# Short convolution in groups of four like tiles: norm groups on 32 partitions, summed and spread by VectorE's block transposes

## The chip, the cores and the metric

The kernel runs on one core of a Trainium2 chip. The metric is the device time of one execution in microseconds (us). Below, PE is TensorE (the matrix engine; PEld its weight loads), DVE is VectorE, ACT is ScalarE, POOL is GpSimd, and SP is SyncE, which here only issues DMAs.

## The reference, cut to what matters

The program is one decoder layer on 256 tokens of width 2048: a mixer, a cross attention to 256 memory tokens, a SwiGLU block, and a final norm. All of it is float32. The change is in the short convolution of the mixer and its grouped norm, which has 16 groups of 128 channels:

```python
def grouped_rmsnorm(x, g, n_groups):
    shp = x.shape
    xf = x.astype(jnp.float32).reshape(shp[:-1] + (n_groups, shp[-1] // n_groups))
    xf = xf * lax.rsqrt(jnp.mean(xf * xf, axis=-1, keepdims=True) + NORM_EPS)
    return (xf.reshape(shp) * g.astype(jnp.float32)).astype(x.dtype)

def hybrid_mixer(h, w_in, ssd_conv_w, ssd_conv_b, dt_bias, a_log, d_skip, ssd_norm,
                 sc_conv_w, sc_norm, w_out):
    proj = h @ w_in
    z, xbc, dt_raw, sc_u, sc_b, sc_c = jnp.split(proj, IN_SPLITS, axis=-1)
    ...
    y_ssd = grouped_rmsnorm(y * jax.nn.silu(z), ssd_norm, SSD_GROUPS)
    v = sc_b * causal_dwconv(sc_c * sc_u, sc_conv_w)
    y_sc = grouped_rmsnorm(v, sc_norm, SC_GROUPS)
    return jnp.concatenate([y_ssd, y_sc], axis=-1) @ w_out
```

`sc_u`, `sc_b` and `sc_c` are 2048 columns each; `causal_dwconv` is a depthwise convolution over three tokens. The other branch (SSD, a state space model) has four norm groups of 512 channels.

## The kernel before

**The weight stream.** All weights come from memory once, in chunks of 128x1024 values (512 KB), in a fixed list (`stream_plan`). SP loads a chunk into a raw tile `r`, up to six ahead (`load_to`). `split_to` makes two tiles of it: ACT rounds it to the tile `h` (line 172, type fp32r), and DVE subtracts to get the rest `l` (line 173). Raw tiles have six buffers, `h` and `l` four each, so the cast of a chunk can start when PE is done with the chunk four before it.

**The projections** (`tok_mm`, lines 260 to 262). Tokens stand on the partitions, 512 output columns on the free axis, in two accumulators of 128 tokens. Three products, h by h, h by l and l by h, make up one float32 product, so that a chunk costs 12 matmuls of 128x512. A `unit` is two chunks. The input projection has 22 groups of 512 columns, each of 8 chunks or 4 units; then comes the output projection of the mixer (stage `wo`, 4 column groups of 16 chunks, in the order of `out_order`), and then attention and SwiGLU, which the change leaves alone.

**Turning a group** (`group_post`). When a group's accumulators are full, DVE transposes them in blocks of 32x32 (`turn_blocks`, line 276), SP writes them to scratch memory (`put`), and SP reads them back (`get`) with channels on the partitions and 256 tokens on the free axis: four tiles of 128 channels. The columns of the weights are permuted on the host (`_turned`) so that each tile gets its own 128 channels.

**Processes.** All work on these tiles is written as Python generators. Once in each unit, between its two chunks, `step` moves every live generator on to its next `yield`. PE and SP execute in exactly this order. DVE, ACT and POOL follow an order that a scheduler makes, which is also fixed when the program is built.

**The short convolution.** `mixer_groups` cuts one list into the 22 groups: tiles of the SSD branch (B, C, z, xs) and of the short convolution (scc, scu, scb) are mixed in a group. For each of the 16 channel tiles, `scu_post` multiplies u by c (line 776) and convolves (lines 778 and 781), and `scb_post` multiplies by b (line 788). One tile is one norm group, so the sum of squares runs over the 128 partitions. `norm_group` with `feature_squares` does it: PE transposes the tile (`flip`, line 207, two transposes of 128x128), ACT squares and sums along the free axis (line 234), DVE scales (line 241), POOL raises to the power -0.5 (line 242), PE spreads the result over the partitions (`bcast`, line 249, two more transposes), DVE multiplies (line 749), and ACT and DVE make the hi and lo halves `ys` (lines 192 and 193) that stage `wo` uses.

The four SSD norm groups use the same `norm_group`, with `feature_sums` in place of `feature_squares`.

Of the kernel before, what the change touches and what calls it, by code (L numbers as in the profile page):

```python
# [13 lines left out]
F32 = mybir.dt.float32  # L14
F32R = mybir.dt.float32r
# [5 lines left out]
T = 256  # L21
# [6 lines left out]
EPS = 1e-5  # L28
# [11 lines left out]
NV = _o  # L40

ZT, XT, BT, CT = 0, 16, 32, 36
UT, SBT, SCT = 0, 16, 32


def mixer_groups():

    o = [("B", "a", BT, 0), ("C", "a", CT, 0), ("z", "a", ZT, 0), ("z", "a", ZT + 1, 1)]
    sc = iter(range(16))

    def short_conv():
        j = next(sc)
        return [("scc", "b", SCT + j, j), ("scu", "b", UT + j, j), ("scb", "b", SBT + j, j)]

    for g in range(4):
        if g:
            o += [("B", "a", BT + g, g), ("C", "a", CT + g, g)]
        for t in range(4 * g, 4 * g + 4):
            if t > 1:
                o.append(("z", "a", ZT + t, t))  # L60
            o.append(("xs", "a", XT + t, t))
            if t % 4:
                o += short_conv()
    for _ in range(4):
        o += short_conv()
    return [o[i:i + 4] for i in range(0, len(o), 4)]
# [28 lines left out]
def trunk(tc, wst, vecs, xp, xtp, mp, wdt_in, nfin, outp):  # L95
# [9 lines left out]
    with ExitStack() as ctx:  # L105
# [25 lines left out]
        def tmp(shape=(128, T)):  # L131
            return tp.tile(list(shape), F32, tag="t", name=nm("t"))
# [69 lines left out]
        def flip(src):  # L202

            ps = msc()
            for i, a in enumerate(src):
                for tb in range(2):
                    nc.tensor.transpose(ps[:, i * T + tb * 128:i * T + tb * 128 + 128],  # L207
                                        a[:, tb * 128:tb * 128 + 128], ident)
            return ps

        def small(name):
            return cp.tile([128, 2], F32, tag=name, name=nm(name), bufs=4)
# [12 lines left out]
                                            axis=mybir.AxisListType.XY, op=ALU.add)  # L225
            return e

        def feature_squares(src):

            ps = flip([src])  # L230
            e = small("rv")
            j = tmp()
            for tb in range(2):
                act(j[:, tb * 128:tb * 128 + 128], ps[:, tb * 128:tb * 128 + 128], AF.Square,
                    accum_out=e[:, tb:tb + 1])
            return e

        def inv_rms(e, n):
            r = small("rr")
            with tc.high_priority():  # L240
                ts(e, e, 1.0 / n, EPS, ALU.mult, ALU.add)  # L241
                gtt(r, e, half, op=ALU.pow)  # L242
            return r

        def bcast(r):
# [18 lines left out]
        def side_blocks(tiles, k0):  # L264

            def blocks(i, tb):
                a = tiles[k0 + i]
                return a[:, tb * 128:tb * 128 + 128], a[:, T + tb * 128:T + tb * 128 + 128]

            return blocks  # L270

# [82 lines left out]

        U = cp.tile([128, T], F32, name="U")
        ident = cp.tile([128, 128], F32, name="ident")
        half = cp.tile([128, 2], F32, name="half")

        c0 = VOFF["nmem"] + 16
        wdt = slot()  # L360
# [5 lines left out]
            dst[i] = t  # L366

        nc.gpsimd.memset(half, -0.5)
        act(small("rv"), half, AF.Identity)
# [371 lines left out]
        def norm_group(items, sums, sq, n, key):  # L741
            r = inv_rms(sums(sq), n)
            yield
            yield
            rb = bcast(r)
            yield
            for src, gain, dst in items:
                y = tmp()
                stt(y, src, gain, rb[:, 0:T], ALU.mult, ALU.mult)  # L749
                ys[dst] = hilo(y)  # L750
                if dst % 2:
                    yield
            done(key)
# [12 lines left out]

        scc, scv = {}, {}

        def scc_post(j, src):
            scc[j] = src  # L770
            return
            yield

        def scu_post(j, src):
            u = tmp()
            tt(runs(u), src, scc.pop(j), ALU.mult)
            a = slot()[:, 0:T]
            ts(a, u, v("sw", 3 * j + 2), None, ALU.mult)
            for k in (1, 0):
                d = 2 - k  # L780
                stt(a[:, d:], u[:, 0:T - d], v("sw", 3 * j + k), a[:, d:], ALU.mult, ALU.add)  # L781
            scv[j] = a
            return
            yield

        def scb_post(j, src):
            a = scv[j]
            tt(runs(a), runs(a), src, ALU.mult)
# [8 lines left out]
        paces = len(groups) - 3  # L797

        def group_post(n, accs):
            t = turn_blocks(accs)  # L800
            yield
            w = put(t)
            yield
            d = get(w)
            yield
            for f, (kind, _, _, j) in enumerate(groups[n]):
                p = posts[kind](j, d[:, f])
                if next(p, 0) is None:
                    procs.append(p)
                if f < 3 and n < paces:  # L810
                    yield

        def in_units(n, accs, cs):
# [7 lines left out]
            for n in range(2):  # L821
                in_units(n, first[n], cs)
        for n in range(2, len(groups)):
            for kind, _, _, j in groups[n]:
                if kind == "B":
                    procs.append(decay(j))
            in_units(n, [acc(), acc()], range(0, KT // 2, 2))


# [67 lines left out]
        def wo_post(n, accs):  # L897
            add_to_res(n, accs, h1s)
            if n == 0:
                act(small("rv"), half, AF.Exp)  # L900
# [312 lines left out]
    return a.reshape((n, 4, 4, 32) + rest).swapaxes(1, 2).reshape((n * 512,) + rest)  # L1213


def _cols(a):

    import numpy as np
    a = np.asarray(a)
    n = a.shape[0] // 128  # L1220
    return a.reshape(n, 128, -1).transpose(1, 0, 2).reshape(128, -1)


def _weights(i):
    import numpy as np
    w_in = np.asarray(i["w_in"])[0]
    blk = {}

# [5 lines left out]
    rows = {m: (_turned(np.asarray(i[k])[0]) if m == "d" else np.asarray(i[k])[0]).reshape(-1, 2, 128, i[k].shape[-1] // 512, 512).transpose(3, 0, 2, 1, 4)  # L1234
            for m, k in (("wo", "w_out"), ("o", "w_o"), ("g", "w_gate"), ("u", "w_up"), ("d", "w_down"))}
    groups = []
    for g in mixer_groups():
        c = np.concatenate([w_in[:, (0 if m == "a" else 5152) + 128 * t:][:, 0:128] for _, m, t, _ in g], axis=1)
        c = _turned(c.T).T
# [24 lines left out]

def _vectors(i):
    import numpy as np
    g = {k: np.asarray(a) for k, a in i.items() if a.ndim <= 3}
    part = {
        "nmix": _cols(g["norm_mix"][0]), "nmem": _cols(g["mem_norm"]), "nxa": _cols(_turned(g["norm_xa"][0], 3)),
        "nffn": _cols(g["norm_ffn"][0]), "nssd": _cols(g["ssd_norm"][0]),  # L1270
        "nsc": _cols(g["sc_norm"][0]), "cw": _cols(g["ssd_conv_w"][0].T), "cb": _cols(g["ssd_conv_b"][0]),
        "sw": _cols(g["sc_conv_w"][0].T), "dsk": _cols(np.repeat(g["d_skip"][0], 64)),
        "dtb": np.broadcast_to(g["dt_bias"][0], (128, H)), "alog": np.broadcast_to(g["a_log"][0], (128, H)),
    }
    return np.ascontiguousarray(np.concatenate([part[n] for n, _ in _W], axis=1))
# [33 lines left out]
```

## Time and profile before

| what | value |
|---|---|
| time, median of three runs | 1533.63 us (1533.0 to 1533.98) |
| the profiled execution's own time | 1533.51 us |
| its span, first to last instruction | 1531.8 us |
| granted TensorE clock, mean | 0.999 |
| DVE busy | 928.7 us (61%) |
| ACT busy | 757.9 us (49%) |
| POOL busy | 52.5 us (3%) |
| mean DMA rate | 221 GB/s |

The profile page gives the busy time of each engine, then the span in 40 slices with a digit for the busy share, then the chain of work that ended last: from the last instruction back, at each step to what released it. Its further parts group the instructions by source line. An engine that is busy 99% of the span sets the time; what the other engines do costs something only where that one waits for them. The input projection of the mixer lies between about 57 and 571 us of the span, stage `wo` up to about 747 us.

### The profile page before, as it was taken

To read this page: it belongs to the slowest core of one execution; us is meant where nothing else is said; L and a number is where in the kernel's file an instruction comes from. 1 tells how busy PE (TensorE), PEld (TensorE's weight loads), DVE (VectorE), ACT (ScalarE), POOL (GpSimd) and SP (SyncE) were. 2 spreads that over 40 slices of the span, in tenths; PEclk is the share of its full clock that TensorE was granted. 3 is DMA by queue.
4 is the path that set the end of the run, shared out by engine and by line. 5 is a ranking of instruction groups with operands and counts; after the bars stand their busy time and mean duration, and the time that the engine had idled before them with its cause. 6 is when DMAs were issued, how large, how long until landed. Compare 5 with 4: busy or idle time off the path is not lost.

```text
span 1531.8 us, 18911 instructions
## 1 busy us (share of the span) xinstructions
PE 1518.1 (99%) x6903; PEld 1246.6 (81%) x6903; DVE 928.7 (61%) x1195; ACT 757.9 (49%) x1070; POOL 52.5 (3%) x65
## 2 busy tenths in 40 slices
PE   8999999999999999999999999999999999999997
PEld 6788888788888888888888888888888888888886
DVE  5958778677777766465575555555555555455453
ACT  6665754754654444454465444444444444344343
POOL 0002200100100000000000000000000000000000
PEclk9999999999999999999999999999999999999999
DMA  9787876877867768587535667666666667655562
GB/s 346 256 270 240 260 229 207 280 217 229 269 214 226 233 206 240 199 262 233 192 132 181 223 216 225 219 203 208 221 222 220 222 217 223 226 194 192 193 193 97
DMA packets 141917, 338.34 MB, mean 221 GB/s; under 512 B 12768, under 2 KB 58240, under 8 KB 141824
## 3 DMA queue, kind: packets, MB, share of 16 engines
q1 hardware_dynamic: 132624, 329.74, 66.7%
q10 hardware_dynamic: 9200, 7.39, 1.6%
q8 instruction: 54, 0.88, 0.3%
q14 instruction: 39, 0.32, 0.1%
HBM read 316.06 MB, written 21.02 MB: 220 GB/s over the span
## 4 chain that ended last, share of the span: by engine, by line
PE 96%; DMA 2%; issue 1%; ACT 1%; DVE 0%; SPq 0%; POOLq 0%; POOL 0%; ACTq 0%
PE a L260 30%; PE a L262 30%; PE a L261 30%; DMA r<-in_w_dram 2%; PE a L342 1%; PE m L717 1%; PE a L348 0%; PE m L207 0%; PE m L249 0%; PE a L556 0%; PE m L876 0%; ACT h L172 0%; PE m L701 0%; PE m L719 0%; PE m L935 0%
## 5 line engine op out<-in xcount | busy, mean ns | idle before, releaser
L173 DVE TENSOR_TENSOR l<-r,h 128x1024 fp32r<-128x1024 f32 (+2 forms) x555 | 658.8, 1190 | 534.4 <-ACT h L172 510.0
L172 ACT CAST h<-r 128x1024 fp32r<-128x1024 f32 (+2 forms) x555 | 566.0, 1023 | 693.6 <-PE a L262 619.1
L260 PE MATMUL a<-h,s 128*128 128x512 f32 x2047 | 805.2, 393 | 0.0
L262 PE MATMUL a<-h,s 128*128 128x512 f32 x2047 | 797.8, 390 | 0.0
L261 PE MATMUL a<-l,s 128*128 128x512 f32 x2047 | 797.7, 390 | 0.0
L262 PEld LDWEIGHTS a<-h,s 128*128 128x128 f32 x2047 | 384.3, 188 | 80.9
L260 PEld LDWEIGHTS a<-h,s 128*128 128x128 f32 x2047 | 384.4, 188 | 80.6 <-issue 2.4
L261 PEld LDWEIGHTS a<-l,s 128*128 128x128 f32 x2047 | 384.6, 188 | 77.7
L242 POOL TENSOR_TENSOR rr<-rv,half 128x2 f32<-128x2 f32 x24 | 23.8, 991 | 574.4 <-DVE rv L241 574.3
L658 DVE SCALAR_TENSOR_TENSOR t<-t,vec,t 128x255 f32<-128x255 f32 (+2 forms) x72 | 33.7, 480 | 0.9
L276 DVE STREAM_TRANSPOSE b<-a 128x512 f32<-128x512 f32 x44 | 29.7, 700 | 2.0 <-PE a L262 1.9
L1132 POOL TENSOR_TENSOR fr<-fr,half 128x1 f32<-128x1 f32 x2 | 1.1, 550 | 716.8 <-DVE fr L1131 716.8
L556 PE MATMUL a<-s,h 128*128 128x512 f32 x64 | 23.9, 404 | 1.4 <-DVE s L187 1.1
L1058 ACT ACTIVATE g<-a,fscale 128x512 f32<-128x512 f32 x22 | 15.0, 689 | 9.9 <-PE a L262 9.9
L557 PE MATMUL a<-s,l 128*128 128x256 f32 x64 | 18.4, 287 | 0.8 <-DVE l L173 0.8
L749 DVE SCALAR_TENSOR_TENSOR t<-s,vec,m 128x256 f32<-128x256 f32 x32 | 14.6, 476 | 4.6 <-PE m L249 4.6
L556 PEld LDWEIGHTS a<-s,h 128*128 128x128 f32 x64 | 12.0, 188 | 5.8 <-DVE s L187 2.3
L342 PE MATMUL a<-s,h 128*128 128x512 f32 x64 | 16.5, 400 | 0.0
L781 DVE SCALAR_TENSOR_TENSOR s<-t,vec,s 128x255 f32<-128x255 f32 (+1 forms) x32 | 16.1, 506 | 0.4
L723 DVE SCALAR_TENSOR_TENSOR s<-s,vec,m 128x256 f32<-128x256 f32 x16 | 7.7, 480 | 14.0 <-PE m L719 13.9
L640 ACT ACTIVATE s<-s,nacs 128x256 f32<-128x256 f32 x32 | 16.0, 499 | 0.0
L1066 DVE SCALAR_TENSOR_TENSOR g<-a,fscale,g 128x512 f32<-128x512 f32 x22 | 15.4, 743 | 0.0
(175 smaller groups left out, 629.3 us busy)
## 6 DMA issues: line engine op xcount, KB each, us to landing
r<-in_w_dram SPq DMA_DIRECT2D x535, 512.0 KB, 4.2
w<-b SPq DMA_DIRECT2D x36, 512.0 KB, 3.3
f<-w SPq DMA_DIRECT2D x144, 128.0 KB, 4.5
s<-acsT ACTq DMA_DIRECT2D x24, 256.0 KB, 6.1
s<-in_xt_dram SPq DMA_DIRECT2D x16, 256.0 KB, 6.4
s<-in_x_dram SPq DMA_DIRECT2D x8, 256.0 KB, 7.6
s<-in_m_dram SPq DMA_DIRECT2D x7, 256.0 KB, 7.2
s<-in_nfin_dram SPq DMA_DIRECT2D x4, 256.0 KB, 6.9
```

The lines of the kernel that those rows point to most:

```text
L172: nc.scalar.copy(h[:, c], r[:, c])
L173: tt(l[:, c], r[:, c], h[:, c].bitcast(F32), ALU.subtract)
L242: gtt(r, e, half, op=ALU.pow)
L260: mm(ps[tb], ah, h[:, w], start=start and i == ks[0], stop=False)
L261: mm(ps[tb], ah, l[:, w], start=False, stop=False)
L262: mm(ps[tb], al, h[:, w], start=False, stop=stop and i == ks[-1])
L276: nc.vector.transpose(t[:, tb * 512:tb * 512 + 512], src[tb])
L342: mm(ps, h[:, k * 128:k * 128 + 128], acts[k0 + k], start=start and k == 0, stop=False)
L556: mm(kacc[t], h[:, t * 128:t * 128 + 128], a, start=s, stop=False)
L557: mm(kacc[t][:, 0:T], l[:, t * 128:t * 128 + 128], a[:, 0:T], start=False, stop=e)
L658: stt(a[:, d:], u[:, 0:T - d], v("cw", 4 * ct + k), a[:, d:], ALU.mult, ALU.add)
L781: stt(a[:, d:], u[:, 0:T - d], v("sw", 3 * j + k), a[:, d:], ALU.mult, ALU.add)
```

## The change

1. **Groups of one kind.** `mixer_groups` now makes 10 groups of SSD tiles and 12 groups of the short convolution, each of four tiles of one kind (scc, scu or scb). Two SSD groups come first, then one of each in turn, and the last four are scb, scc, scu, scb. The SSD order within its groups is as before apart from the cut.
2. **Norm groups on 32 partitions.** The columns of the short convolution's groups are no longer permuted on the host. The block transposes then leave norm group b of the four on partitions 32b to 32b+31 of all four tiles. The gains, the convolution's weights and the rows of `w_out` are permuted to match (`_sc_turned`).
3. **Four tiles at a time.** Products, squares, casts and differences of the short convolution take two tiles in one instruction (128x512); the convolution itself and the gains stay at 128x256.
4. **Sums and spreading without PE.** For four tiles together, DVE adds the squares of the four tiles, transposes the sum in blocks of 32x32, and reduces over each 32 columns, which gives 128x8 sums; POOL raises them to -0.5 in one instruction; DVE transposes them back, broadcast, which gives the factor for each token and norm group on its 32 partitions. `feature_squares` is gone, and with it 32 transposes on PE, and the 32 of `bcast` for these groups.
5. **Order of `wo`.** The first two column groups leave chunks 6, 7, 14 and 15 for last, where they left 14 and 15 before.

```diff
-            yield
-            yield
-            yield from norm_group([(a, v("nsc", j), 16 + j)], feature_squares, a, 128, ("sc", j))
+            sq = []
+            for i in range(2):
+                a, ar = pair(scv[n][i])
+                tt(ar, ar, src[:, 2 * i:2 * i + 2], ALU.mult)
+                q = gtp.tile([128, 512], F32, tag="g", name=nm("q"))
+                act(q, a, AF.Square)
+                sq.append(q)
+            yield
+            tt(sq[0], sq[0], sq[1], ALU.add)
+            s = tmp()
+            tt(s, sq[0][:, 0:T], sq[0][:, T:], ALU.add)
+            t = tmp()
+            nc.vector.transpose(t, s)
+            e = cp.tile([128, 8], F32, tag="ge", name=nm("ge"), bufs=2)
+            nc.vector.tensor_reduce(e, runs(t), axis=mybir.AxisListType.X, op=ALU.add)
+            ts(e, e, 1.0 / 128, EPS, ALU.mult, ALU.add)
+            r = cp.tile([128, 8], F32, tag="gr", name=nm("gr"), bufs=2)
+            gtt(r, e, half, op=ALU.pow)
+            yield
+            rb = tmp()
+            nc.vector.transpose(runs(rb), r.unsqueeze(2).to_broadcast([128, 8, 32]))
+            for i in range(2):
+                y = gtp.tile([128, 512], F32, tag="g", name=nm("y"))
+                for f in range(2):
+                    c = slice(f * T, f * T + T)
+                    stt(y[:, c], scv[n][i][:, c], v("nsc", 4 * n + 2 * i + f), rb, ALU.mult, ALU.mult)
+                hi, lo = slot(dt=F32R), slot(dt=F32R)
+                nc.scalar.copy(hi, y)
+                tt(lo, y, hi.bitcast(F32), ALU.subtract)
...
 def out_order():
-    return ([(n, c) for n in range(2) for c in range(14)] + [(n, c) for n in range(2) for c in (14, 15)]
+    late = (6, 7, 14, 15)
+    return ([(n, c) for n in range(2) for c in range(KT) if c not in late] + [(n, c) for n in range(2) for c in late]
             + [(n, c) for n in (2, 3) for c in range(KT)])
```

**On PE**, before, between two chunks of the seventeenth group of the input projection; `a` are the accumulators, `s_639` and `s_678` halves of the normed input, and the row of line 249 is the spreading of one norm group's factor:

```order
L260 MATMUL a_4117<-h_4249,s_639 128x512
L261 MATMUL a_4117<-l_4250,s_639 128x512
L262 MATMUL a_4117<-h_4249,s_639 128x512
L249 MATMUL m_4290<-ident,rr_4196 128x128 x2
L260 MATMUL a_4116<-h_4253,s_678 128x512
L261 MATMUL a_4116<-l_4254,s_678 128x512
L262 MATMUL a_4116<-h_4253,s_678 128x512
```

On PE, after the change, at the same place (lines 242 to 244 are now the three products):

```order
L242 MATMUL a_4027<-h_4137,s_639 128x512
L243 MATMUL a_4027<-l_4138,s_639 128x512
L244 MATMUL a_4027<-h_4137,s_639 128x512
L242 MATMUL a_4026<-h_4141,s_678 128x512
L243 MATMUL a_4026<-l_4142,s_678 128x512
L244 MATMUL a_4026<-h_4141,s_678 128x512
```

The two transposes are gone and the chunks follow on each other. Over the whole program PE has 46 transposes of line 207 and 44 of line 249 before, and 14 and 12 (lines 199 and 231) now; the other matmuls are the same in number.

**On DVE**, before, at about the same place; the row of line 241 scales the sums `rv` that POOL then takes, and that of line 749 uses the factor of the same norm group once PE has spread it; `l` are the halves of weight chunks:

```order
L241 TENSOR_SCALAR rv_4192<-rv_4192 128x2
L173 TENSOR_TENSOR l_4254<-r_4167,h_4253 128x1024
L723 SCALAR_TENSOR_TENSOR s_3917<-s_3917,vec,m_4239 128x256
L173 TENSOR_TENSOR l_4303<-r_4221,h_4302 128x1024
L726 TENSOR_TENSOR s_3917<-s_3917,s_3873 128x256
L734 TENSOR_TENSOR s_3637<-s_3637,t_4287 128x256
L173 TENSOR_TENSOR l_4307<-r_4223,h_4306 128x1024
L658 SCALAR_TENSOR_TENSOR t_4296<-t_4294,vec,t_4296 128x255
L658 SCALAR_TENSOR_TENSOR t_4296<-t_4294,vec,t_4296 128x254
L749 SCALAR_TENSOR_TENSOR t_4348<-s_4033,vec,m_4290 128x256
```

On DVE, after the change, for the third set of four tiles (chunk 160 or so of 176); `q` are the squares, `ge` the sums, `gr` what POOL makes of them, and line 165 is the split of a weight chunk:

```order
L790 TENSOR_TENSOR q_4773<-q_4773,q_4776 128x512
L792 TENSOR_TENSOR t_4820<-q_4773 128x256
L794 STREAM_TRANSPOSE t_4822<-t_4820 128x256
L796 TENSOR_REDUCE ge_4824<-t_4822 128x8
L165 TENSOR_TENSOR l_4786<-r_4708,h_4785 128x1024
L797 TENSOR_SCALAR ge_4824<-ge_4824 128x8
L802 STREAM_TRANSPOSE t_4869<-gr_4827 128x256
L687 TENSOR_TENSOR s_4629<-m_4778,dtn 128x256
L807 SCALAR_TENSOR_TENSOR y_4871<-s_4383,vec,t_4869 128x256
L165 TENSOR_TENSOR l_4834<-r_4756,h_4833 128x1024
```

Where three splits and five other rows stood between the scaling and the use of the factor, line 802, which reads POOL's result, now stands directly behind line 797, which gives POOL its input. It is the same for the fourth set; for the first set one split, and for the second one block transpose and one split stand between the two.

More of the change, by code (lines that the diff above doesn't have):

```diff
@@ L356, in trunk @@
         ident = cp.tile([128, 128], F32, name="ident")
[L357 removed]
+        half = cp.tile([128, 8], F32, name="half")
         c0 = VOFF["nmem"] + 16
@@ L767, in trunk, with pair, scc_post @@
         scc, scv = {}, {}
-        def scc_post(j, src):
-            scc[j] = src
+        def pair(a):
+            return a, a.rearrange("p (f x j) -> p f x j", f=2, x=8)
+        def scc_post(n, src):
+            scc[n] = src
             return
             yield
[L774 to L783, printed above, removed]
-            yield
@@ L805, in group_post @@
             yield
-            for f, (kind, _, _, j) in enumerate(groups[n]):
+            if isinstance(groups[n], tuple):
+                yield from posts[groups[n][0]](groups[n][1], d)
+                return
+            for f, (kind, _, j) in enumerate(groups[n]):
                 p = posts[kind](j, d[:, f])
@@ L823, in trunk @@
         for n in range(2, len(groups)):
-            for kind, _, _, j in groups[n]:
-                if kind == "B":
-                    procs.append(decay(j))
+            for one in [] if isinstance(groups[n], tuple) else groups[n]:
+                if one[0] == "B":
+                    procs.append(decay(one[2]))
             in_units(n, [acc(), acc()], range(0, KT // 2, 2))
@@ L899, in wo_post @@
             if n == 0:
-                act(small("rv"), half, AF.Exp)
+                act(small("rv"), half[:, 0:2], AF.Exp)
             if n == 3:
```

84 lines of the change are left out of this document (45 added, 39 removed).

## The prediction

> **What bounds the kernel now.** I read the page's head, its slices and its chain first, then the waits of PE alone, then the windows.
>
> ```profile
> span 1531.8 us, 18911 instructions
> ...
> PE 1518.1 (99%) x6903; PEld 1246.6 (81%) x6903; DVE 928.7 (61%) x1195; ACT 757.9 (49%) x1070; POOL 52.5 (3%) x65
> ...
> PE   8999999999999999999999999999999999999997
> ...
> PE 96%; DMA 2%; issue 1%; ACT 1%; DVE 0%; SPq 0%; POOLq 0%; POOL 0%; ACTq 0%
> ```
>
> PE is busy in every slice, and the chain that ends last runs on PE for 96% of the span. A high busy share can still hide stalls, so the next view is the list of what PE waited for (total us, times, longest):
>
> ```profile
> PE m L401 <- POOL U L397: 1.8, 1, 1.8
> PE a L556 <- DVE s L187: 1.1, 2, 0.6
> PE a L557 <- DVE l L173: 0.8, 2, 0.6
> PE m L954 <- ACT s L192: 0.6, 1, 0.6
> PE a L556 <- ACT h L172: 0.3, 1, 0.3
> PE m L565 <- ACT h L172: 0.3, 1, 0.3
> PE m L566 <- DVE l L173: 0.2, 1, 0.2
> ```
>
> These are the start of the program (L397 to L567) and attention (L954). No line of the input projection or of stage wo (L260 to L262, L207, L249) is in it. The windows view says the same, as busy time of PE, PEld, DVE, ACT and POOL in a stretch:
>
> ```profile
> 100.00:613.00 513.00, 513.00 (x2375) 416.10 (x2374) 372.96 (x555) 283.07 (x450) 44.47 (x46) 1.00 0.76 237
> 820.00:1260.00 440.00, 440.00 (x1943) 364.43 (x1942) 234.44 (x222) 194.51 (x203) 0.00 (x0) 1.00 0.67 217
> ```
>
> Where the change works, PE is full at granted clock 1.00, and DVE is busy 73% (373 of 513). So a PE instruction less is time less, as long as no other engine comes to hold PE up. The second row is SwiGLU alone, all chunk matmuls: 440/1943 = 0.2264 us from one to the next, and 12 of them, a chunk, last 2.72 us.
>
> **What leaves PE.** The views of the two lines give their count and duration (ns, least/median/most):
>
> ```profile
> L249 PE MATMUL m<-ident,rr x44: 270/272/273, 34.7 to 613.1; 128*128 128x128 f32 x44
> L207 PE MATMUL m<-ident,s x44: 270/272/331, 156.7 to 601.7; 128*128 128x128 f32 x44
> ```
>
> Of each 44, the 16 norm groups of the short convolution own 32; the four SSD groups keep 8, and 4 more serve the input and memory norms. So 64 transposes go, in 32 pairs. What a pair costs is not its duration, since matmuls overlap, but how far it pushes the next chunk matmuls. One pair in the timeline of PE (start, duration):
>
> ```profile
> 421.15 0.39 PE L262 MATMUL a<-h,s 128*128 128x512 f32 x1
> 421.38 0.38 PE L249 MATMUL m<-ident,rr 128*128 128x128 f32 x2
> 421.51 0.48 PE L260 MATMUL a<-h,s 128*128 128x512 f32 x1
> 421.83 0.39 PE L261 MATMUL a<-l,s 128*128 128x512 f32 x1
> ```
>
> Without the pair, L260 and L261 would start 0.226 and 0.453 us after L262, the latter at 421.60. It starts at 421.83: 0.23 us for the pair. The chain of waits agrees, for a pair and for two pairs together:
>
> ```profile
> 310.22 0.22 PE m L249 x2
> ...
> 601.56 0.44 PE m L207 x4
> ```
>
> So 32 pairs cost between 32 x 0.22 = 7.0 and 32 x 0.24 = 7.7 us, the latter if the next matmuls also lose a hundredth or two. I take 0.225 each: **-7.2 us**. Nothing is added on PE.
>
> A rule of the Trainium skill would price this otherwise: "TensorE: Matmul & The Clock Gate", Part 4: PE-mode transpose, gives about 275 ns for a 128x128 transpose within a kernel. This trace's median of 272 ns agrees as a duration; by it as a price the sum would be 64 x 0.275 = 17.6 us, but the 0.11 us that the chain shows for each decides here.
>
> **What comes to DVE, ACT and POOL.** Rows by form (busy us, mean ns):
>
> ```profile
> L173 DVE TENSOR_TENSOR l<-r,h 128x1024 fp32r<-128x1024 f32 x518 | 634.8, 1227 | 519.1 <-ACT h L172 495.5 <-DMA r<-in_w_dram 17.8 <-DMA f<-w 3.1
> L172 ACT CAST h<-r 128x1024 fp32r<-128x1024 f32 x518 | 544.8, 1053 | 672.7 <-PE a L262 609.1 <-issue 27.8 <-DMA r<-in_w_dram 20.6
> L276 DVE STREAM_TRANSPOSE b<-a 128x512 f32<-128x512 f32 x44 | 29.7, 700 | 2.0 <-PE a L262 1.9
> L685 DVE TENSOR_TENSOR s<-s,s 128x512 f32<-128x512 f32 x16 | 10.9, 681 | 0.0
> L193 DVE TENSOR_TENSOR s<-t,s 128x256 fp32r<-128x256 f32 x32 | 12.8, 419 | 0.1
> L749 DVE SCALAR_TENSOR_TENSOR t<-s,vec,m 128x256 f32<-128x256 f32 x32 | 14.6, 476 | 4.6 <-PE m L249 4.6
> L221 DVE TENSOR_REDUCE rv<-m 128x2 f32<-128x256 f32 x4 | 1.7, 422 | 0.6 <-PE m L207 0.5
> L234 ACT ACTIVATE t<-m 128x128 f32<-128x128 f32 x32 | 8.5, 270 | 5.0 <-PE m L207 5.0
> ```
>
> DVE did seven 128x256 instructions and a small one for each tile, about 7 x 0.46 + 0.2 = 3.4 us, 13.7 for four tiles. Now four tiles take seven of 128x512 (0.68 each, 4.8), seventeen of 128x256 (0.42 to 0.48, 7.8), and two half-size transposes, a reduction and a small one (0.35 + 0.35 + 0.42 + 0.2 = 1.3): 13.9. That is no more work over the stage. ACT loses the 32 squarings of L234, done two tiles at a time instead. Neither sum is on the path, because both engines run ahead of PE: the cast of a chunk waits for PE (609 of ACT's 673 us of idle time), since h and l have four buffers each. From that moment PE still has three chunks, 8.2 us, and the cast and the split take 1.05 + 1.23, so a split is ready **5.9 us** before its use. That lead is the cover, and it is gone only if DVE falls back by more.
>
> **The new wait.** DVE's block transpose L802 now stands behind POOL's power of 128x8, close behind the row that feeds POOL, and the splits are queued behind it. The trace has that operation at one and two columns:
>
> ```profile
> L1132 POOL TENSOR_TENSOR fr<-fr,half 128x1 f32<-128x1 f32 x2 | 1.1, 550 | 716.8 <-DVE fr L1131 716.8
> L242 POOL TENSOR_TENSOR rr<-rv,half x24: 688/691/1839, 32.2 to 806.9; 128x2 f32<-128x2 f32 x24
> ```
>
> A second column adds 0.14 us, so eight give 0.55 + 7 x 0.14 = 1.5 us, which I take. The ends are 0.7 (eight columns cost what two do) and 4 x 1.84 = 7.4 (four times a disturbed one). I count DVE's work in the new order with the durations above. The densest place is the first set: among seven splits in a row (7 x 1.23 = 8.6) stand 8 of the 0.48 kind, 5 of 0.68, 7 of 0.42, two whole block transposes and two halves, a reduction and the feeding row (12.9 in all), and the power, beside which one of the splits runs, adds 1.5 - 1.2 = 0.3. That makes 21.8 us, while PE uses seven chunks in 19.0: DVE falls back by 2.8, or by 4.0 if the split has to wait for POOL. At the third set, whose rows stand with the change, nothing runs beside the power: four splits (4.9), 6.8 of other work and 1.5 make 13.2, PE's four chunks 10.9, so 2.3. All of these are under 5.9. The power would have to take 1.5 + 5.9 - 4.0 = 3.4 us at the first set or 1.5 + 5.9 - 2.3 = 5.1 at the third before PE waits; about 4.4 is the mean for the four. So I cost the wait at **nothing**.
>
> That the split might have to wait shows in these two rows of one moment (start, duration), and in the longest split of the stage (ns, least/median/most of all its forms):
>
> ```profile
> 346.05 1.22 DVE L173 TENSOR_TENSOR l<-r,h 128x1024 fp32r<-128x1024 f32 x1 [0.16 <-DMA f<-w]
> 346.06 1.76 POOL L242 TENSOR_TENSOR rr<-rv,half 128x2 f32<-128x2 f32 x1 [15.70 <-DVE rv L241]
> L173 DVE TENSOR_TENSOR l<-r,h x555: 418/1224/2315, 5.3 to 1513.5; 128x1024 fp32r<-128x1024 f32 x173, 128x512 fp32r<-128x512 f32 x11, 128x256 fp32r<-128x256 f32 x1
> ```
>
> Beside a split the power took 1.76 instead of 0.69 us: about a split's length more. The Trainium skill, "SBUF — State Buffer", section SBUF: two separate sides, states why: a DVE instruction with two SBUF inputs and a GpSimd instruction that reads SBUF exclude each other for their whole length. It speaks against this change, and the trace agrees; with the rule the sum stays, and the first rival below is a little likelier.
>
> **What is moved.** SP issues the same chunks, puts and gets; only four loads of the residual move by a few chunks, and they are used when a column group of wo ends. Stage wo needs the last tiles of the short convolution at its 14th unit; they are made from the 4th to the 7th after their group. The last SSD tiles come about 19 units after their group, 4 of them in wo, and are needed at the 13th. Each is over 5 units of 5.4 us early.
>
> **Sum.** The profiled execution took 1533.51 us (1531.8 and 1.7 around it), 0.1 under the median of the runs. 1533.5 - 7.2 = **1526.3 us**. For the likeliest case alone: 1525.5 to 1527.0.
>
> **The rivals.**
> - *The wait comes through in part.* If the power takes 4 to 5.5 us, or DVE's order meets a wait that I did not count, PE waits 0.5 to 4 us in all: 1526.8 to 1530.3. For it: the lead is half used up at the first set already. Against: 0.14 us a column. Chance 0.10.
> - *Slower: POOL's power takes four disturbed ones, 7.4 us.* The four sets then hold PE for some 7.4 - 4.4 = 3.0 us each: 12.0 - 7.2 = +4.8, 1538.3 us. It turns slower than before from 4.4 + 1.8 = 6.2 us for the power on (7.2 / 4 = 1.8 us of wait at each set). For it: eight columns are four times two. Against it: at the last two sets DVE stands still during the power, so nothing disturbs it there. Chance 0.04.
> - *The weight stream is the real bound*, and PE only gains waits for chunks: no change, 1533.5 us. For it: a DMA share of 0.76 in the stage. Against it: of ACT's idle time before 518 casts, 20.6 us are put down to chunks that had not landed, 609 to PE. Chance 0.07.
> - *A transpose costs its duration*, 272 ns: 64 x 0.272 = 17.4, 1516.1 us. Against it: the timeline above. Chance 0.02.
>
> **How the numbers follow.** The forecast has 0.77. The range reaches from 1525.0, a pair at 0.24 and half a us of spread as in the runs, to 1530.3, the end of the first rival. 0.2% is 3.1 us, about what a measurement of this kernel can tell from no change. Faster by more: the forecast, the first rival and the last, 0.89. Within: 0.07. Slower: 0.04.
>
> **What would show it.** Right: PE with 64 instructions fewer, still without a wait in the stage, and the power near 1.5 us. The pair's price is right if the stage's end comes 7 us earlier. Wrong: chunk matmuls in the list of PE's waits, released by DVE's split, near the four powers; then the wait is the step that failed. If PE gains waits on ACT's cast that a chunk released, it was the stream. Wrong in size: no such wait, but a gain other than 7.0 to 7.7.

## The result

| kernel | time, median | runs, lowest to highest | ratio to before, 95% interval |
|---|---|---|---|
| before | 1533.61 us | 1533.0 to 1533.98, 4 runs | 1 |
| changed | 1525.83 us | 1525.64 to 1526.01, 4 runs | 0.995 (0.9932 to 0.9967) |

The change made the kernel 7.8 us faster. The profiled execution took 1525.64 us; its span is 7.9 us shorter than that of before. The forecast was 1526.3 us.

The page of the changed kernel, with the lines that answer to those of before:

```profile
span 1523.9 us, 18600 instructions
...
PE 1511.2 (99%) x6839; PEld 1241.5 (81%) x6839; DVE 931.0 (61%) x1179; ACT 751.0 (49%) x1004; POOL 44.5 (3%) x53
...
PE 96%; DMA 2%; issue 1%; ACT 1%; DVE 0%; SPq 0%; POOLq 0%; POOL 0%; ACTq 0%
```

PE has 64 instructions fewer and is busy 6.9 us less, and the chain that ends last still runs on PE for 96% of the span. DVE's total hardly moved. What PE waits for in the changed kernel (total us, times, longest):

```profile
PE m L384 <- POOL U L380: 1.8, 1, 1.8
PE a L540 <- DVE l L165: 0.8, 2, 0.6
PE a L539 <- DVE s L179: 0.8, 2, 0.5
PE m L978 <- ACT s L184: 0.6, 1, 0.6
```

Lines 380 to 540 are the start of the program, and line 978 is attention, as before. None of lines 242 to 244, the chunk matmuls, is in the list: the new wait of DVE for POOL did not come through. The windows of the same two stretches (busy time of PE, PEld, DVE, ACT and POOL):

```profile
100.00:613.00 513.00, 513.00 (x2345) 416.44 (x2345) 380.08 (x546) 279.83 (x388) 36.84 (x34) 1.00 0.77 240
820.00:1260.00 440.00, 440.00 (x1943) 364.44 (x1942) 234.68 (x222) 194.05 (x204) 0.00 (x0) 1.00 0.67 218
```

PE is still full in the stage of the change, at granted clock 1.00, and SwiGLU is as before to the instruction. So the gain is PE work that is no longer there. Where it was gained shows in the first chunk matmul behind attention, in the timeline of PE of the changed kernel:

```profile
767.05 0.59 PE L242 MATMUL a<-h,s 128*128 128x512 f32 x1
```

and of the kernel before:

```profile
774.88 0.59 PE L260 MATMUL a<-h,s 128*128 128x512 f32 x1
```

By then 774.88 - 767.05 = 7.8 us have been gained, which is all of it. At the first chunk of stage `wo` it was 6.4 us (564.35 against 570.75), since the last norm groups are worked on inside `wo`.

The new operations by their lines: duration in ns, least/median/most, then what DVE waited for in front of line 802:

```profile
L799 POOL TENSOR_TENSOR gr<-ge,half x4: 1637/1638/2545, 244.2 to 586.8; 128x8 f32<-128x8 f32 x4
...
  DVE t L802: 5.2, 3
```

POOL's power of 128x8 takes 1.64 us, where the prediction took 1.5. DVE does stand still for it, 5.2 us in all at three of the four sets. Nothing of that reaches PE.

### The profile page after: what moved, and what is told of

Same layout as the page of the kernel before. It is cut to its first block, busy times and chain, and to the rows that moved or that the text cites. A ratio compares the mean times of both kernels' runs of the same rounds, so it can differ in the third digit from the quotient of the medians.

```text
span 1523.9 us, 18600 instructions
## 1 busy us (share of the span) xinstructions
PE 1511.2 (99%) x6839; PEld 1241.5 (81%) x6839; DVE 931.0 (61%) x1179; ACT 751.0 (49%) x1004; POOL 44.5 (3%) x53
## 4 chain that ended last, share of the span: by engine, by line
PE 96%; DMA 2%; issue 1%; ACT 1%; DVE 0%; SPq 0%; POOLq 0%; POOL 0%; ACTq 0%
PE a L242 31%; PE a L243 30%; PE a L244 30%; DMA r<-in_w_dram 2%; PE a L325 1%; PE m L700 1%; PE a L331 0%; PE a L539 0%; PE m L900 0%; ACT h L164 0%; PE m L684 0%; PE m L702 0%; PE m L959 0%; PE a L540 0%; PE m L990 0%
## 5 line engine op out<-in xcount | busy, mean ns | idle before, releaser
L242 PE MATMUL a<-h,s 128*128 128x512 f32 x2047 | 802.5, 392 | 0.0
L243 PE MATMUL a<-l,s 128*128 128x512 f32 x2047 | 797.2, 389 | 0.0
L244 PE MATMUL a<-h,s 128*128 128x512 f32 x2047 | 797.0, 389 | 0.0
L242 PEld LDWEIGHTS a<-h,s 128*128 128x128 f32 x2047 | 384.3, 188 | 81.8 <-issue 2.6
L244 PEld LDWEIGHTS a<-h,s 128*128 128x128 f32 x2047 | 384.3, 188 | 80.3
L243 PEld LDWEIGHTS a<-l,s 128*128 128x128 f32 x2047 | 384.4, 188 | 78.3
L224 POOL TENSOR_TENSOR rr<-rv,half 128x2 f32<-128x2 f32 x8 | 8.3, 1035 | 469.8 <-DVE rv L223 469.8
L1101 DVE TENSOR_TENSOR s<-f,s 128x512 fp32r<-128x512 f32 x22 | 14.2, 685 | 1.3 <-ACT s L1100 1.3
L540 PEld LDWEIGHTS a<-s,l 128*128 128x128 f32 x64 | 12.6, 197 | 2.5 <-DVE l L165 2.1
```

The costliest lines, as they stand in the source:

```text
L242: mm(ps[tb], ah, h[:, w], start=start and i == ks[0], stop=False)
L243: mm(ps[tb], ah, l[:, w], start=False, stop=False)
L244: mm(ps[tb], al, h[:, w], start=False, stop=stop and i == ks[-1])
L540: mm(kacc[t][:, 0:T], l[:, t * 128:t * 128 + 128], a[:, 0:T], start=False, stop=e)
```

## The experiments

The kernels ran in three sets, each on a chip of its own and with its own runs of the kernel before. In the first set (the e1, e2 and e3 kernels) that took 1533.09 us. In the second (e4_power_x5 and the two e5 kernels) it took 1533.05, and the changed kernel 1525.31. In the third (e4_power_x3, e6 and e7) it took 1532.95, and the changed kernel 1525.25. Differences "to the changed kernel" use 1525.31 for the first two sets, though it did not run in the first, and 1525.25 for the third. All are medians.

The theory: the gain is the 64 transposes on PE, at 0.11 to 0.12 us each, and everything that is new on DVE and POOL is hidden by the lead of the weight splits. The main rival: the gain, or part of it, comes from the new grouping and order.

### The transposes put back: e1_pairs_back

The changed kernel with 32 pairs of transposes that nothing reads, one pair in a unit after each scb group:

```diff
+        def unread(pairs):
+            for _ in range(pairs):
+                ps = msc()
+                for tb in range(2):
+                    nc.tensor.transpose(ps[:, tb * 128:tb * 128 + 128], ident, ident)
+                yield
...
+            procs.append(unread(8))
```

> The changed kernel with 64 transposes of 128x128 put back on PE, in 32 pairs between chunks, of the identity and read by nobody. If the change gains by PE's instructions alone (a pair at 0.22 to 0.24 us), 7.0 to 7.8 us come back: 1532.8 to 1533.6. If it gains by the new grouping or by the batched work on DVE and ACT, the time stays at 1525.8. If a transpose costs its duration of 272 ns, 1543.2.

Measured: 1533.07 us (10 runs), ratio to before 1.0001 (0.9992 to 1.001). The whole gain is gone, 7.76 us over the changed kernel, so 0.24 us for a pair. One pair of this kernel in the timeline of PE (`x2` are its two transposes):

```profile
275.23 0.39 PE L244 MATMUL a<-h,s 128*128 128x512 f32 x1
275.46 0.38 PE L784 MATMUL m<-ident 128*128 128x128 f32 x2
275.60 0.48 PE L242 MATMUL a<-h,s 128*128 128x512 f32 x1
275.91 0.40 PE L243 MATMUL a<-l,s 128*128 128x512 f32 x1
```

Without the pair, L243 would start 2 x 0.226 us after L244, at 275.68; it starts at 275.91. That is the 0.23 us that the prediction read from the kernel before, though each of these transposes is on record with a median of 0.27 us.

### Twice as many at the same places: e1b_two_fold

The same, with `range(4)` in place of `range(2)`. It tells a price for each transpose from a price for each break in the row of chunk matmuls.

> As the run with the pairs put back, but four transposes at each of the 32 places. If each transpose has its own price (0.11 to 0.12 us), 14 to 15.5 us are added to the changed kernel: 1539.9 to 1541.3. If it is the break in the run of chunk matmuls that costs, it is as with pairs, about 1533.2.

Measured: 1540.19 us, ratio to before 1.0048 (1.0033 to 1.0062). The second 64 transposes cost 1540.19 - 1533.07 = 7.1 us, 0.111 each, the first 64 0.121. Nearly all of the price is the transpose itself; the break adds about a hundredth of a us for each.

### The old order without the transposes: e2_before_no_turns

The kernel before, with its old groups of four kinds, its tile at a time and its order, but without these 64 transposes; ACT squares the tile itself and a constant takes the place of the spread factor, so that this norm is left out.

```diff
-            ps = flip([src])
...
-                act(j[:, tb * 128:tb * 128 + 128], ps[:, tb * 128:tb * 128 + 128], AF.Square,
+                act(j[:, tb * 128:tb * 128 + 128], src[:, tb * 128:tb * 128 + 128], AF.Square,
...
-            rb = bcast(r)
+            rb = U if key[0] == "sc" else bcast(r)
```

> The kernel before, in its old grouping, without the 64 transposes of the short convolution's norm: ACT squares the tile itself instead of the transposed one, and the factor is taken from a constant, so that this norm is left out; DVE, ACT and POOL keep their instructions. If PE's instructions are the whole gain: 1533.6 less 7.2 to 7.8, 1525.8 to 1526.4. If the regrouping is needed for it: near 1533.6.

Measured: 1525.16 us, ratio to before 0.9951 (0.9934 to 0.9968), 7.9 us faster. Without the new groups, the four-tile instructions or the new order of `wo`, the gain is the same as that of the whole change (1525.31) within the spread of the runs. The rival that the order brings something falls. DVE, ACT and POOL keep their instructions in this kernel, so their work is not what was gained either.

### Four tiles at a time, but turned on PE: e3_pe_once

The changed kernel, but with the sum of four tiles turned, and its factor turned back, by PE: 16 transposes, a pair of pairs for each set, in place of DVE's block transposes.

```diff
-            t = tmp()
-            nc.vector.transpose(t, s)
+            yield
+            t = flip([s])[:, 0:T]
...
-            rb = tmp()
-            nc.vector.transpose(runs(rb), r.unsqueeze(2).to_broadcast([128, 8, 32]))
+            w = tmp()
+            nc.vector.tensor_copy(runs(w), r.unsqueeze(2).to_broadcast([128, 8, 32]))
+            yield
+            rb = flip([w])[:, 0:T]
+            yield
```

> The changed kernel, but the sum of four tiles is turned and its factor spread by PE, once for four tiles: 16 transposes instead of none, and 64 before. If the price is per transpose (0.115 to 0.12 us): 1525.8 + 1.9 = 1527.7, which is to say that doing four tiles at once brings 5.8 of the 7.8 us and the block transposes on DVE 1.9. If it is the block transposes on DVE that matter: near 1533.6.

Measured: 1527.07 us, ratio to before 0.9962 (0.9949 to 0.9975); 1.8 us over the changed kernel, for 8 pairs 0.22 each. In the profiles it is 2.0 us, 0.25 each (the table further below). So of the 7.8 us, some 5.8 to 6.0 come from one turn for four norm groups in place of four, and 1.8 to 2.0 from taking that turn off PE.

### The power made longer: e4_power_x3 and e4_power_x5

The lead of a split is the time between its end and its first use on PE. In the changed kernel it is mostly 5.8 to 7.2 us. Among the splits queued behind line 802 it is 4.4 us at the first set, 5.9 at the second, 4.3 at the third and 3.8 at the fourth, as taken from the rows of DVE and PE. If this lead is what hides DVE's wait for POOL, a power longer by less than 3.8 us costs nothing, and a longer one costs what is over at each set.

```diff
-            gtt(r, e, half, op=ALU.pow)
+            for _ in range(5):
+                gtt(r, e, half, op=ALU.pow)
```

The other kernel has `range(3)`.

> The changed kernel with POOL's power done three times over: DVE waits 4.9 us for it, 3.3 more than now, at each of the four sets. The splits behind it are 4.4, 5.9, 4.3 and 3.8 us early in the changed trace. If the lead is the cover, all of it is still hidden: 0 to 0.5 us more than the changed kernel, and no chunk matmul among PE's waits. If PE waited for part of every delay, 3.3 / 6.6 of what five powers cost (9.3 us): 4.6 us.

> The changed kernel with POOL's power done five times over, so that DVE's block transpose waits 5 x 1.64 = 8.2 us for it at each of the four sets, 6.6 more than now. If the lead of the splits is the cover, PE now begins to wait: in the changed trace the splits behind the wait are still 4.4, 5.9, 4.3 and 3.8 us early, so 2.2 + 0.7 + 2.3 + 2.8 = 8 us are added. If DVE's wait is hidden whatever its length, 0. If none of it is hidden, 4 x 6.6 = 26 us.

Measured: three times (4.9 us of power) 1525.33 us, 0.1 over the changed kernel, ratio to before 0.995 (0.9937 to 0.9964), and no chunk matmul in PE's waits. Five times (8.2 us) 1534.61 us (10 runs, 1533.24 to 1538.05), 9.3 over the changed kernel, ratio to before 1.0012 (1.0002 to 1.0021). PE's waits in the latter begin with

```profile
PE a L243 <- DVE l L165: 7.4, 4, 2.5
```

Four waits, one at each set (2.39, 0.81, 1.68 and 2.49 us, where 2.2, 0.7, 2.3 and 2.8 were expected), and the line that waits is the one that uses the split `l`: this is the picture that the prediction gave for the case of its failure. They add up to 7.4 us of the 8.0 expected. The profiled execution (1535.24 us) is 10 us over the changed kernel, so some 2.5 us are not in the waits. Most of them are here, in the timeline of PE behind the first of the four:

```profile
251.84 0.39 PE L242 MATMUL a<-h,s 128*128 128x512 f32 x1
254.62 0.76 PE L243 MATMUL a<-l,s 128*128 128x512 f32 x1 [2.39 <-DVE l L165]
255.17 0.63 PE L244 MATMUL a<-h,s 128*128 128x512 f32 x1
255.60 0.63 PE L242 MATMUL a<-h,s 128*128 128x512 f32 x1
256.03 0.63 PE L243 MATMUL a<-l,s 128*128 128x512 f32 x1
...
257.73 0.57 PE L244 MATMUL a<-h,s 128*128 128x512 f32 x1
258.14 0.40 PE L242 MATMUL a<-h,s 128*128 128x512 f32 x1
258.38 0.39 PE L243 MATMUL a<-l,s 128*128 128x512 f32 x1
```

and in the windows before, in and behind that stretch (the third number from the end is the granted clock):

```profile
250.00:253.00 3.00, 2.23 (x10) 1.50 (x8) 0.00 (x0) 0.00 (x0) 2.90 (x2) 1.00 0.54 85
254.60:257.00 2.40, 2.38 (x6) 1.92 (x7) 2.40 (x5) 1.44 (x3) 0.00 (x0) 0.52 0.50 177
259.50:262.00 2.50, 2.50 (x16) 1.95 (x13) 2.50 (x4) 1.54 (x3) 0.00 (x0) 1.00 0.65 220
```

After the wait of 2.39 us PE ran at about half its clock for some 3.4 us: matmuls 0.43 us apart in place of 0.227. The eight steps from 254.62 to 258.14 took 3.52 us instead of 1.81, 1.7 us lost on top of the wait. The rest is PE's restart. A wait is counted from the end of the matmul before it, 0.39 us behind that one's start, where without a wait the next would have started after 0.23: another 0.16 us at each wait. And behind the other three waits the second matmul comes 0.33 us after the first in place of 0.23, as here at the fourth:

```profile
604.25 0.50 PE L243 MATMUL a<-l,s 128*128 128x512 f32 x1 [2.49 <-DVE l L165]
604.58 0.39 PE L244 MATMUL a<-h,s 128*128 128x512 f32 x1
604.81 0.39 PE L242 MATMUL a<-h,s 128*128 128x512 f32 x1
```

Together 7.4 + 1.7 + 4 x 0.16 + 3 x 0.1 = 10.0 us, all that this execution has over the changed kernel. The median is 9.3 over it, and the four fastest of the ten runs (1533.24 to 1533.52) are 7.9 to 8.2 over it.

### A near miss that was not forecast: e5_dve_tight, e5_dve_loose, e6_dve_tight12

The lowest leads of the changed kernel are not at the powers. They are at about 147 to 153 us, behind the first SSD tiles. These rows of DVE come first, start and duration:

```profile
137.89 2.31 DVE L165 TENSOR_TENSOR l<-r,h 128x1024 fp32r<-128x1024 f32 x1
...
142.04 1.45 DVE L668 TENSOR_TENSOR s<-s,s 128x512 f32<-128x512 f32 x1
143.41 1.52 DVE L670 TENSOR_TENSOR s<-s,s 128x256 f32<-128x256 f32 x1
...
145.78 1.22 DVE L165 TENSOR_TENSOR l<-r,h 128x1024 fp32r<-128x1024 f32 x1
...
150.72 1.83 DVE L165 TENSOR_TENSOR l<-r,h 128x1024 fp32r<-128x1024 f32 x1
```

and here PE takes the last two of these splits:

```profile
147.71 0.39 PE L243 MATMUL a<-l,s 128*128 128x512 f32 x1
...
153.15 0.39 PE L243 MATMUL a<-l,s 128*128 128x512 f32 x1
```

147.71 - 147.00 and 153.15 - 152.55: these splits are 0.7 and 0.6 us early. For the same two chunks the kernel before has 3.2 and 3.0. Two things stand in the rows. Between the split that ends at 140.20 and that of 145.78, DVE does other products without a break for 5.6 us, some of them stretched from 0.68 and 0.42 to 1.45 and 1.52 us beside POOL:

```profile
141.48 3.16 POOL L399 TENSOR_TENSOR s<-s,s 128x512 f32<-128x512 f32 x2
```

And ACT makes no cast between 137.35 and 143.72, since the exponentials of the decay and another function take turns there, with three loads of ACT's tables of 1.28 us:

```profile
137.37 1.28 ACT L623 ACT_TABLE_LOAD   x1
...
139.18 1.28 ACT L642 ACT_TABLE_LOAD   x1
...
141.43 1.28 ACT L625 ACT_TABLE_LOAD   x1
...
143.72 1.98 ACT L164 CAST h<-r 128x1024 fp32r<-128x1024 f32 x2
```

The kernel before has stretched products at this time as well, but no table load, and its splits stand between the products. If this reading holds, more work for DVE at this place costs time beyond the small lead, and the same work elsewhere nothing.

```diff
+            if t == 0:
+                w = slot()
+                for _ in range(6):
+                    tt(w[:, 0:T], U, U, ALU.mult)
```

Six products of 128x256, 2.5 us, are added to the changed kernel behind the first SSD tile (tight, about 142 us) or, with `t == 12`, behind the thirteenth (loose; they ran at 472 to 478 us, where the smallest lead of the changed kernel is 3.3 us); in the third kernel `range(12)`, 5.0 us, behind the first.

> The changed kernel with six products of 128x256 more on DVE (2.5 us), read by nobody, behind the first tile of the SSD branch, about 142 us into the span. There the changed trace has splits only 0.7 and 0.6 us before PE needs them. If the lead is what counts, PE waits there about 1.9 us and the time grows by that. If DVE's total work or its busy share counts, as much as with the same six products elsewhere. If nothing on DVE counts, 0.

> The same six products behind the thirteenth tile of the SSD branch, about 485 us into the span, where the changed trace has the splits 5 to 7 us early. If the lead is what counts: 0, to within 0.3 us. If DVE's total work counts: as much as in the other place.

> Twelve products of 128x256 (5.0 us) instead of six behind the first tile of the SSD branch, where six gave 0.5 to 4.5 us in single runs and no wait in the profiled one. If the lead there, 0.7 us or a little more, is what counts: PE waits 2.5 to 4.3 us for a split, and the time is 1528 to 1530, or above where the clock drops behind the wait. If the spread with six products had another cause than the lead: no wait of PE on a split, 1525 to 1526.

Measured: loose 1525.71 us, 0.4 over the changed kernel, a little more than the 0.3 expected; its profile has no wait of a chunk matmul, and its runs (1525.24 to 1525.88) overlap those of the changed kernel (1524.77 to 1525.56). Tight 1528.32, 3.0 over it, but its runs lie between 1525.82 and 1529.77, and the profiled one, the fastest of them, has no wait for a split: the smallest lead there was 0.7 us, with POOL's additions at other moments. So the six products do not settle the amount. Twelve do: 1529.47 us (10 runs), ratio to before 0.9979 (0.997 to 0.9989), 4.2 us over the changed kernel, and PE's waits begin with

```profile
PE a L243 <- DVE l L165: 4.1, 2, 2.5
```

5.0 us more of work and 4.1 us of waits: about 0.9 us was covered at this place, of the size of the 0.6 and 0.7 us read from the trace. The figure is rough, since some of the products were stretched too (the longest took 1.51 us). That this place is tight is shown; how much of it is ACT's table loads and how much DVE's products rests on the rows alone, since no run took the loads away.

### The same for the SSD norm groups: e7_ssd_too

A search for a better version. The four SSD norm groups have 512 channels, four tiles of 128, so their sums need all partitions. Here DVE makes 128x8 sums as in the short convolution, and PE adds them over the four blocks of 32 partitions by one small matmul with a matrix of zeros and ones; DVE spreads the factor. 16 more transposes go, and 4 matmuls of 128x8 come.

```diff
-            r = inv_rms(sums(sq), n)
...
-            rb = bcast(r)
+            t = tmp()
+            nc.vector.transpose(t, sq)
+            e = small8("ge")
+            nc.vector.tensor_reduce(e, runs(t), axis=mybir.AxisListType.X, op=ALU.add)
...
+            mm(ps[:, 0:8], same, e, start=True, stop=True)
...
+            rb = tmp()
+            nc.vector.transpose(runs(rb), r.unsqueeze(2).to_broadcast([128, 8, 32]))
```

> The changed kernel with the four norm groups of the SSD branch done in the same manner: block transposes on DVE, and one small matmul on PE each that adds the sums of the four quadrants, in place of 16 transposes. At 0.115 to 0.12 us a transpose, 1.9 us go and four small matmuls of 128x8 come, 0.1 to 0.25 each with the break: 0.9 to 1.5 us less than the changed kernel. If the four further waits of DVE on POOL reach PE: as fast as the changed kernel or slower.

Measured: 1525.22 us, ratio to before 0.995 (0.9937 to 0.9962): no difference to the changed kernel (1525.25). The small matmul is not small on PE:

```profile
L740 PE MATMUL m<-ge,same x8: 174/215/256, 226.5 to 560.7; 128*128 128x8 f32 x8
```

Each of the four runs as two instructions, and pushes the chunk matmuls behind it by 0.24 us, like a pair of transposes. Of two pairs for each group one is gained, 4 x 0.24 = 1.0 us. But a chunk matmul is now among PE's waits, once:

```profile
PE a L246 <- DVE l L165: 0.3, 1, 0.3
```

It stands at 339.75 us, behind the second SSD norm group. DVE waits there for POOL's power and then has a row of products, so that the next split is late:

```profile
332.29 0.45 DVE L747 STREAM_TRANSPOSE t<-gr 128x256 f32<-128x256 f32 x1 [1.82 <-POOL gr L744]
...
338.52 2.32 DVE L165 TENSOR_TENSOR l<-r,h 128x1024 fp32r<-128x1024 f32 x2
```

In the changed kernel the split for this chunk is 3.9 us early. With its restart the wait costs PE 0.6 us: the matmul before it starts at 339.05, the waiting one at 339.75 and the next at 340.09, 0.70 and 0.34 us in place of 0.23 each. So 0.4 of the 1.0 us is left. The profiles agree: from the first chunk matmul of the input projection to the last L245 of stage `wo` (L242 in the changed kernel) there are 680.27 us here, and 680.70 in the changed kernel's run of the same set. An effect of 0.4 us cannot be seen in runs that lie up to 1.6 us apart. So the second case of the expectation came true in part: at one of the four groups the new work on DVE used up the lead. That it was the wait for POOL, more than the products around it, rests on these rows alone.

## Why the prediction was right

**The bound.** PE sets the time, with no waits in the stage, so that a PE instruction less is time less. It held, from both sides: the old order without its 64 transposes is 7.9 us faster, and 64 put back into the changed kernel make it 7.8 us slower. The profiles show it more sharply than the times of the runs. These are the starts, in us, of the first chunk matmul of the input projection and of the first one behind attention:

| kernel | first | behind attention | between |
|---|---|---|---|
| before | 57.41 | 774.88 | 717.47 |
| changed | 57.27 | 767.05 | 709.78 |
| e1_pairs_back | 58.01 | 775.43 | 717.42 |
| e2_before_no_turns | 56.17 | 765.92 | 709.75 |
| e3_pe_once | 56.69 | 768.47 | 711.78 |
| e4_power_x3 | 57.36 | 767.11 | 709.75 |
| e5_dve_loose | 57.50 | 767.29 | 709.79 |

The old order without the transposes and the new order agree to within 0.03 us, so the grouping, the four-tile instructions and the order of `wo` bring nothing on balance. Longer powers and more products on DVE do not show either, as long as the lead covers them.

**What leaves PE.** 32 pairs was the right count. The term that was mis-sized is the price of a pair: 0.225 us was taken, 0.24 was measured (7.76 / 32). The prediction had 0.24 as its upper bound, for a hundredth or two that the next matmuls also lose; they do lose it. Its own row of the timeline had given 0.23 already. With 0.24 the sum is 1525.8 us, the median of the changed kernel. The price by duration, 64 x 0.272 = 17.4 us, is excluded by both e1 kernels. The lower end of the range holds a slip: a pair at 0.24 and half a us of spread give 1525.3 us, not 1525.0. Nothing hung on it.

**What comes to DVE, ACT and POOL.** "No more work over the stage" held on the whole: DVE's total rose by 2.3 us (928.7 to 931.0) and ACT's fell by 6.9. What DVE gained is largely the same instructions taking longer. The splits by form, changed kernel:

```profile
L165 DVE TENSOR_TENSOR l<-r,h 128x1024 fp32r<-128x1024 f32 x518 | 637.7, 1233 | 509.3 <-ACT h L164 478.7 <-DMA r<-in_w_dram 26.5 <-DMA f<-w 2.4
...
L668 DVE TENSOR_TENSOR s<-s,s 128x512 f32<-128x512 f32 x16 | 12.1, 758 | 0.0
```

They are 518 and 16 as before, and take 1233 and 758 ns where they took 1227 and 681. The prediction counted only the short convolution's work and looked for danger only at the four sets. It did not see that the moved SSD tiles would bring the lead down to 0.6 us elsewhere. That cost nothing here, but by only 0.6 us, while a single stretched split (2.31 in place of 1.22) takes 1.1 us more. That no wait came up at this place was luck as far as the prediction goes, and this was its weakest step.

**The new wait.** The power took 1.64 us against the 1.5 estimated, 0.95 more than with two columns, 0.16 for a column. That POOL would be slowed by a split beside it at the first set was right. The rows of POOL:

```profile
244.23 2.54 POOL L799 TENSOR_TENSOR gr<-ge,half 128x8 f32<-128x8 f32 x1 [19.63 <-DVE ge L797]
```

and of DVE:

```profile
244.06 1.22 DVE L165 TENSOR_TENSOR l<-r,h 128x1024 fp32r<-128x1024 f32 x1
246.81 0.45 DVE L802 STREAM_TRANSPOSE t<-gr 128x256 f32<-128x256 f32 x1 [1.53 <-POOL gr L799]
```

The split from 244.06 to 245.28 lies beside the power, which took 2.54 us in place of 1.64, 0.9 more; the prediction had reckoned with a split's length, 1.2, by which one of the two has to wait. The Trainium skill, "SBUF — State Buffer", section SBUF: two separate sides, says that two such instructions exclude each other; this trace agrees, and the rule changed nothing in the time, since the lead was there.

**The lead as cover.** It was right that nothing comes through, and the lead of 5.9 us that was worked out is also the median in the changed trace, over the 240 chunks of the two stages. The limits were set too low. The prediction had PE waiting from a power of 3.4 us at the first set and 4.4 us in the mean; with 4.9 us nothing came through at any of the four. From the leads of the changed kernel the limits are 1.64 + 3.8 = 5.4 us at the tightest set and 1.64 + 4.6 = 6.2 us in the mean; with a power of 4.9 us the trace of e4_power_x3 still has 0.3 us at the tightest set, a split that ends at 597.25 and is used at 597.52. The turn to "slower than before", forecast at a power of 6.2 us, lies at about the 8.2 us of e4_power_x5 (ratio 1.0012). The reason seems to lie in the sum of work at the first set, which was made as if all of it fell behind one moment: in the trace it is spread, and the lowest lead there is 2.9 us, of a split before the power, where 5.9 - 2.8 = 3.1 was expected behind it. No run tested this.

**The rivals.** The wait in part is what the longer powers show, but only from beyond 4.9 us. The slower case needed a power of 7.4 us. The weight stream as the bound falls with e1 and e2: PE takes up the freed 7.8 us in full, and no wait for a chunk is new in its list.

## What to carry to other kernels

Where PE is full and the others run ahead, a PE instruction that is taken away is worth what it pushes the next ones by, read from the starts in the timeline, and not its duration: 0.12 us for a float32 transpose on record with 0.27. Most of the gain here came from doing the turn once for four norm groups (some 5.8 to 6.0 of 7.8 us); moving that one turn to an engine with room brought the rest. Before and after a change of order, list the smallest leads of the hidden work over the whole stage and not only at the changed place: the tightest one here, 0.6 us, was where tiles had only been moved, and in e7_ssd_too the added work on DVE used up one of 3.9 us.

## What was not expected of the hardware

**A wait can cost more than its length.** Every wait here cost some 0.27 us more than its listed length, for PE's restart. And behind a wait of 2.39 us PE's granted clock was 0.52 for some 3.4 us, 1.7 us lost (e4_power_x5). Behind the wait of 2.49 us later in the same execution it was not, as the rows from 604.25 on show (the granted clock from 604.00 to 607.50 was 1.00), nor behind one of 2.47 us in e6_dve_tight12.

The Trainium skill, "TensorE: Matmul & The Clock Gate", Part 1: The HAM clock gate, tells of a half rate after an idle window of about 3.4 us, in windows that run freely. The length of the slow stretch agrees; that a wait of under 3.4 us brings it on at one time and not at another is what these runs add. It would fit the wide spread of e4_power_x5's runs (1533.24 to 1538.05), though only one of them has a profile: the mean granted clock listed for them is 0.998 in the four fastest, 0.997 in the next five and 0.996 in the slowest. In e6_dve_tight12 the two do not go together (its slowest run, 1532.66 us, has 0.999), so the cause of the spread stays open.

**DVE and POOL stretch each other.** Three of DVE's rows at 138 to 143 us took 2.31, 1.45 and 1.52 us in place of 1.22, 0.68 and 0.42, with POOL's instructions beside them. Where they meet may differ from one execution to the next: e5_dve_tight, in which the lead there was all but used up, has five runs that lie 4 us apart, and in its one profile the stretched rows were others than in the changed kernel's. In e5_dve_loose, which adds nothing at this place, the smallest lead there was 0.2 us (a split that ends at 147.72, used at 147.93) in place of 0.6.
